# Expert weights in 16 KB runs, and expert outputs combined as gated float32r pairs

## The chip, the cores and the metric

The kernel runs on one core of a Trainium2 chip. The metric is the device time of one execution in microseconds (us), as the median of three runs.

## The reference

256 tokens of 1024 channels, float32, go through two blocks of two layers each. The first block's layers have two attention branches and a feed-forward part; the second block's layers have a mixer (retention, differential attention, gated linear attention) and then a mixture of experts, which is where the change acts:

```python
N_EXPERTS = 32
TOP_K = 2
D_EXPERT = 512
...
    def expert_block(args):
        toks, gts, e = args
        xb = h_pad[toks]
        u = jax.nn.silu(xb @ w_gate[e]) * (xb @ w_up[e])
        return (u @ w_down[e]) * gts[:, None].astype(xb.dtype)
```

Each token goes to two of 32 experts. An expert has a gate and an up matrix of 1024 x 512 and a down matrix of 512 x 1024. Its output rows are multiplied by the tokens' gates and added up for each token.

## The kernel before

**Weights.** All weights come through eight slots of 16 KB per partition, 2 MB each. `add` lists the tiles in the order of use, `pump` issues their DMAs on SyncE's queue (SP) in that order as long as a slot is free, and `done(name)` gives a slot back when the last product of a tile stands on TensorE (PE). `reserve(n)` holds n slots back. An expert's gate, up and down matrix are one tile each: w_eg, w_eu and w_ed in the trace. The source of each is laid out by `kp` (L592), "(k p) n -> p k n": partition p gets rows p, 128 + p, 256 + p and so on. So a partition's 16 KB come as eight runs of 2 KB (gate, up) or four runs of 4 KB (down).

**Experts in pairs.** `second_moe` goes through 16 pairs of experts. Each expert has 64 places, so the places of a pair fill 128 partitions. The two experts of a pair run side by side in the two column halves of PE's array. In the loop over i, PE's work stands in this order: the gate products of pair i (`two("g", ...)`), `combine` of pair i-1, the up products, `place` for pair i+1, and the down products.

**place.** `hot(i)` makes a one-hot matrix of tokens and places, once times the norm's factor of each token (`on`) and once times the gates (`ohg`). `place` gathers the tokens: for each of eight chunks of 128 channels, and for two halves of the tokens, it loads a 128 x 128 block of x as the stationary matrix and moves `on` through it. Here x is read by `x_chunk(t, k)`, 128 channels that lie side by side. Then two transposes turn `ohg` into `oT`. Between the two halves of the gathers stand four transposes of `u_`, the hidden activations of pair i (`turn_u`, L1958).

**combine.** `evac_y` (L1815, L1816) copies the pair's two output banks to SBUF, one on ScalarE (ACT) and one on VectorE (DVE), and `combine` multiplies them by `oT` in float32, four products of 128 x 512, into four banks that hold the sum over all pairs. The last pair's outputs are multiplied by a gain first and added on top.

**Past the places.** Ahead of pair 8 (`PAST`), `past_places` runs a loop (L1841) over blocks of tokens that found no place; in it the experts' weights are fetched by tiles of its own, OV, whose gathers use `oh`. In the profiled execution layer 0's loop has no pass and layer 1's has one.

**How it appears in the trace.** A float32 product is two instructions on PE, each with a weight load of its own (PEld); a float32r product is one. Buffers of the same pool share names: `qwh` holds placed tokens, `qwl` the outputs on their way to the combination, `C` stands for constants (the identity, ones), `bank` for PSUM. `macc` holds sums of modulation columns, which `mod_tail` turns by products with one column of ones.

Of the kernel before, what the change touches and what calls it, by code (L numbers as in the profile page):

```python
# [67 lines left out]
def constants():  # L68
# [20 lines left out]
    for lv in range(7):  # L89
# [27 lines left out]
       ("kv_a_norm_g", 2), ("b_gate", 16), ("norm1_g_2", 8), ("norm2_g_2", 8), ("b_mod_2", 48),  # L117
# [17 lines left out]
def build(ctx, tc, I, out, cols, cols2, dbg=None):  # L135
# [16 lines left out]
    def warm(n):  # L152
        """keeps the tensor engine's clock up through a wait on other engines"""
        p = bank()
        for _ in range(n):
            mm(p[:, :128], ident, ident, True, True)
# [11 lines left out]
    # ---- slots of 16 KB per partition: weights in the order of use, and large work tiles  # L168
# [11 lines left out]
    def pump():  # L180
        while st["issued"] < len(stream) and st["live"] + max(st["work"], st["reserve"]) < NSLOT:
            name, src, k, n, split = stream[st["issued"]]
            t = big.tile([128, k, n], F, name="w_" + name, tag="slot", bufs=NSLOT)
            if split == "turns":
                # a pair's two tiles in parts, by turns
# [7 lines left out]
            else:  # L193
                # the very first in parts, so that its products start early
# [27 lines left out]
    # ---- weights as float32r pairs, a few parts ahead of their products  # L222
# [71 lines left out]
    def tok_part(name, kk, c0, c1, ah, al, k, outs, start, stop):  # L294
        """outs[t] += A[t-th 128 rows] @ W[kk, c0:c1]; A is held transposed (ah + al)."""
        wh, wl = gran(name, kk, c0)
        n = c1 - c0
        for t in range(2):
            mm3(outs[t], ah[:, k, t * 128:(t + 1) * 128], al[:, k, t * 128:(t + 1) * 128],
                wh[:, :n], wl[:, :n], start, stop)  # L300

    def chan_part(name, kk, c0, c1, bh, bl, k, banks, start, stop):
        """banks hold [128 channels, 2, 256 tokens]; one 128-wide chunk of W after another."""
# [9 lines left out]
    # ---- constants and small parameters  # L313
# [55 lines left out]

    def load_c():  # L370
        return load_col(I["c_2"])
# [17 lines left out]
    # ---- pieces  # L389
# [8 lines left out]
    def rstd(ss, n, late=False):  # L398
# [6 lines left out]
        # from the exponent's half, three steps of Newton  # L405
# [15 lines left out]
    def to_pair(hi, lo, src, scale=None):  # L421
        """src (PSUM or SBUF) times a column or constant, as a float32r pair."""
# [11 lines left out]
    def norm_steps(src, dg, n, hi, lo, A, B=None):  # L434
        """hi + lo [128, chunk, 256] = (rows of src, times diag) transposed, times A (plus B)."""
# [26 lines left out]
    def x_stats(steps=False):  # L462
        """1 / rms of x's rows, or the steps to it"""
# [19 lines left out]
    def x_hat(dst):  # L483
        """x normed without gain, as chunks"""
# [10 lines left out]

    def row_of(r):
        """[128, 2], token 128t + p at [p, t] -> the row of 256 on every partition."""
# [7 lines left out]
    def bcast_row(col):  # L505
        """[128, 8] with channel 128k + p at [p, k] -> the row of 1024 on every partition."""
# [12 lines left out]
    class Post:  # L519
        """x += rmsnorm(acc) * gain, one half of the columns after the other; acc[t][half] are banks."""  # L520
# [12 lines left out]
        def add(self, sq=None):  # L533
            """sq: acc still lacks this factor of each row."""
# [26 lines left out]
    def mod_tail(keep=0):  # L561
        while len(mod_late) > keep:
            l, s, acc = mod_late.pop(0)
            p = bank()
            for c in range(4):
# [25 lines left out]
    # ---- the order of the weights  # L591
# [55 lines left out]
    # ---- softmax attention, units of [128 queries, 2, 256 keys]  # L647
# [59 lines left out]
    def first_layer(l):  # L707
# [5 lines left out]
        # the norm's factor of each row is left out here and multiplied in after the products  # L713
# [17 lines left out]
        for i, a, b in IN_TILES:  # L731
# [3 lines left out]
            for k in range(8):  # L735
# [8 lines left out]
                if i == 0 and k == 3:  # L744
                    # the latents, transposed as pairs; their norms' factors come after their products
# [23 lines left out]
        # grouped attention: norms of q and k and their rotary, on 10 heads of 64  # L769
# [31 lines left out]
        # up projections of the latents  # L801
# [26 lines left out]
        free(1)  # CT  # L828
        # rotary parts of the latent heads: 8 of q, one of k
# [17 lines left out]
        # gates  # L847
# [36 lines left out]
        # grouped attention: pairs of heads (p, p + 4), keys block-diagonal over the two kv heads  # L884
# [94 lines left out]
        free(1)  # M1  # L979
        drain()  # L980
        # branches, channels on partitions
# [38 lines left out]
        free(1)  # MG  # L1020
# [5 lines left out]
        # feed forward, 512 hidden channels at a time; the norm's factor r of each row is left out of its  # L1026
        # input and multiplied in after it, as r * r
# [54 lines left out]
    # ---- second block  # L1082
# [6 lines left out]
    def load_second():  # L1089
        nc.sync.dma_start(router, kp(I["router_w_2"]))  # L1090
# [4 lines left out]
    # rotary tables of the positions  # L1095
# [7 lines left out]
    def tables():  # L1103
# [8 lines left out]
        # the routing's bias plus the half of sigmoid(z) = tanh(z / 2) / 2 + 1/2  # L1112
# [49 lines left out]
    def stream_second(l):  # L1162
# [7 lines left out]
        for i in range(NE // 2):  # L1170
            for nm, src, k, n in (("g", I["w_gate_2"], 8, 512), ("u", I["w_up_2"], 8, 512), ("d", I["w_down_2"], 4, 1024)):
                for e in (2 * i, 2 * i + 1):
                    add("e%s%d_%d" % (nm, l, e), kp(src[l, e]), k, n, "turns" if nm in TURNS and i == NE // 2 - 1 else None)

    def head_norm(src, g, e, gate, dest):
        """dest = rmsnorm over e of src [128, g, e] times gate, in three pieces."""
# [18 lines left out]
    def silu_gate(src, gain, dest):  # L1195
        """dest [128, 512] = silu(src) * gain, for a gain given as its half, in two pieces."""
# [8 lines left out]
    def second_mix(l):  # L1205
# [10 lines left out]
        # ---- gated linear attention: projections  # L1216
# [31 lines left out]
        # gains of the differential heads: on the turned dimensions in the rotary tables, on the others  # L1248
        # with the transposition
# [27 lines left out]
        # log decay per token and channel  # L1277
# [24 lines left out]
        # gates times gains, ahead of their use  # L1302
# [10 lines left out]
        def qk_evac(s):  # L1313
            """q or k of the differential heads, normed and turned."""
# [24 lines left out]
        # decays of the levels  # L1339
# [78 lines left out]
        # ---- gated linear attention: scores level by level  # L1418
# [56 lines left out]
        # retention beside it, its tiles where q and k of the differential heads were  # L1475
# [98 lines left out]
        free(1)  # HT  # L1574
        drain()
        # ---- output projection, a pair of chunks after another as they come
# [21 lines left out]
        free(2)  # c2, DA  # L1598
# [4 lines left out]
        dve.scalar_tensor_tensor(a2, ms(4), 1.0, V(l, "norm2_g_2"), op0=OP.add, op1=OP.mult)  # L1603
# [14 lines left out]
        free(2)  # MX, MT  # L1618
# [4 lines left out]
    def list_past(cnt, pl3, wg3, nblk_i, eid_i, ov):  # L1623
        # an expert's blocks: one for each CAP tokens begun past the first CAP, at most three
# [31 lines left out]
    def second_moe(l):  # L1656
# [5 lines left out]
        def turn(k0, on_act):  # L1662
            p = bank()
            for k in (k0, k0 + 1):
                for t in range(2):
                    o = (k - k0) * 256 + t * 128
                    pe.transpose(p[:, o:o + 128], x_chunk(t, k), ident)  # L1667
# [20 lines left out]
        def quarter(tag):  # L1688
            """2 KB; the buffers that hold parts of weights elsewhere"""
            return wk.tile([128, 512], F, name="q" + tag, tag=tag, bufs=NSPLIT)  # L1690
        # ---- routing
# [59 lines left out]
        # ---- places: how many earlier tokens chose the same expert  # L1751
# [14 lines left out]
        # ---- tokens past an expert's 64 places: blocks of 64, listed by expert  # L1766
# [3 lines left out]
        def hot(i):  # L1770
            """one-hot of the pair's 2 x 64 places, times the norm's factors and times the gates."""
# [9 lines left out]
            return on, og  # L1781

        def place(oh, og, between=None):
            """the placed tokens, normed, modulated and transposed; the gated places, transposed."""
            hg = []
            for k0 in (0, 4):
# [3 lines left out]
                for k in range(k0, k0 + 4):  # L1790
                    o = p[:, (k - k0) * 128:(k - k0 + 1) * 128]
                    for t in range(2):
                        mm(o, x_chunk(t, k), oh[:, t], t == 0, t == 1)
# [9 lines left out]
            for t in range(2):  # L1803
                pe.transpose(p[:, t * 128:(t + 1) * 128], og[:, t], ident)  # L1804
            oT = t2((128, 2, 128), name="oT")
            act.activation(oT, p[:, :256].rearrange("p (t q) -> p t q", t=2), AF.Copy)
            return hg, oT

        def evac_y(py, last=False):
            y = [quarter("wl"), quarter("wl")]  # L1810
            if last:
                for h in range(2):
                    dve.tensor_tensor(y[h], py[h], g2_[:, h * 512:(h + 1) * 512], op=OP.mult)
                return y
            act.activation(y[0], py[0], AF.Copy)  # L1815
            dve.tensor_copy(y[1], py[1])  # L1816
# [4 lines left out]
        def combine(i, oT, y):  # L1821
            """the sum over the experts stays in four banks; the last pair's comes on top of it"""
            if not acc:
                acc.extend([bank(), bank()] for _ in range(2))
            for h in range(2):
                sl = slice(h * 512, (h + 1) * 512)
                for t in range(2):
                    if i < NE // 2 - 1:
                        mm(acc[t][h], oT[:, t], y[h], i == 0)
                        continue  # L1830
                    c = bank()
                    mm(c, oT[:, t], y[h], True, True)
# [4 lines left out]
        def past_places():  # L1837
            """the blocks past the places, one expert at a time"""
            OV = [slot("OV", [128, 2, 2048]) for _ in range(2)]
            nblk = nc.values_load(nblk_i[0:1, 0:1], min_val=0, max_val=NBLK - 1)  # L1840
            with tc.For_i(0, nblk, 1) as iv:  # L1841
# [3 lines left out]
                # 64 places; even chunks of the width go through the array's left half, odd ones through the  # L1845
                # right, and the halves are added as they are transposed
# [191 lines left out]
```

## Time and profile before

| what | value |
|---|---|
| three runs, us | 2164.03, 2168.88, 2169.59 |
| median, us | 2168.88 |
| profiled execution, us (its span) | 2165.9 |
| PE busy | 2056.2 us, 95% |
| DVE, ACT, GpSimd busy | 46%, 35%, 11% |
| DMA | 620.85 MB, mean 287 GB/s |

The span is that of one execution taken with the profiler; no other time is given for that execution. The share of busy time is an average: the first block's layers are bound by PE alone, while in the expert stages (971 to 1449 us and 1646 to 2149 us of the span) DMA moves weights all the time too.

### The profile page before, as it was taken

Reading aid. Unit: us, or ns where it says so; the run is one execution under the profiler, and the core shown is the slowest. Engines: PE = TensorE matmul, PEld = TensorE weight load, DVE = VectorE, ACT = ScalarE, POOL = GpSimd, SP = SyncE. Lnnn points to the kernel's source line nnn. Section 1 sums busy time; section 2 is a strip of 40 time slices with the busy share of each in tenths; the row PEclk is TensorE's granted clock in tenths of the full one; section 3 lists DMA queues with packets and bytes.
Section 4 is the critical chain, followed back from the end, with each engine's and each line's share of the span. In section 5 each row is a group of like instructions: output and inputs, shape, how many; then the busy total and the mean of one; then the engine's idle time right before and its main releaser. Section 6 shows DMA issues by size and latency. Waiting matters only on the chain. (4 is left out here: it accounts for less than half of the span.)

```text
span 2165.9 us, 28855 instructions
## 1 busy us (share of the span) xinstructions
PE 2056.2 (95%) x11394; PEld 1365.7 (63%) x11394; DVE 993.0 (46%) x1867; ACT 766.4 (35%) x1595; POOL 249.0 (11%) x309
## 2 busy tenths in 40 slices
PE   8999999999999989999999599998999999779999
PEld 6888999788899877774444244436685444333443
DVE  5767878776788867762110011115775111101112
ACT  6555655665565555431111011105452111101110
POOL 1211000021100014420000000002521000000000
PEclk9999999999999999999999799999999999989999
DMA  6545877454568732479999999994457999989998
GB/s 226 210 156 196 308 283 279 173 194 148 202 221 319 271 135 78 146 282 350 393 395 394 351 395 392 393 392 166 156 195 278 391 395 395 392 307 395 395 391 328
DMA packets 269950, 620.85 MB, mean 287 GB/s; under 512 B 9691, under 2 KB 14709, under 8 KB 269557
## 3 DMA queue, kind: packets, MB, share of 16 engines
q1 hardware_dynamic: 268660, 614.78, 76.4%
q10 hardware_dynamic: 1152, 4.20, 0.5%
q8 instruction: 91, 1.49, 0.3%
q14 instruction: 47, 0.38, 0.0%
HBM read 617.91 MB, written 1.05 MB: 286 GB/s over the span
## 5 line engine op out<-in xcount | busy, mean ns | idle before, releaser
L150 PE MATMUL bank<-U,wh 128*128 128x256 f32 x1536 | 287.5, 289 | 0.5 <-DVE U L428 0.4
L150 PE MATMUL bank<-w_eg,qwh 128*64 128x512 f32 x1024 | 230.2, 596 | 29.8 <-DMA w_ed<-in_w_down 25.4
L150 PEld LDWEIGHTS bank<-U,wh 128*128 128x128 f32 x1536 | 239.9, 190 | 8.4 <-issue 5.3
L150 PE MATMUL bank<-w_ed,uT 128*64 128x512 f32 x1024 | 229.6, 598 | 2.4 <-DMA w_ed<-in_w_down 2.1
L150 PE MATMUL bank<-w_eu,qwh 128*64 128x512 f32 x1024 | 227.4, 595 | 0.0
L150 PE MATMUL bank<-U,wl 128*128 128x256 f32 x768 | 218.6, 285 | 4.8 <-DVE wl L269 4.8
L1799 ACT ACTIVATE qwh<-bank,modc,a 128x128 f32<-128x128 f32 x128 | 58.5, 457 | 384.7 <-PE bank L150 354.0
L150 PEld LDWEIGHTS bank<-w_eg,qwh 128*64 128x64 f32 x1024 | 74.3, 138 | 179.5 <-issue 170.5
L150 PEld LDWEIGHTS bank<-w_eu,qwh 128*64 128x64 f32 x1024 | 77.1, 137 | 145.1 <-issue 138.3
L150 PE MATMUL bank<-wh,H 128*128 128x512 f32 x512 | 163.9, 395 | 0.0
L150 PEld LDWEIGHTS bank<-w_ed,uT 128*64 128x64 f32 x1024 | 71.3, 137 | 137.2 <-issue 133.3
L150 PE MATMUL bank<-wh,HT 128*128 128x512 f32 (+1 forms) x448 | 155.7, 402 | 0.6 <-ACT wh L257 0.6
L150 PEld LDWEIGHTS bank<-U,wl 128*128 128x128 f32 x768 | 146.0, 190 | 6.2 <-DVE wl L269 6.0
L150 PEld LDWEIGHTS bank<-on,x 128*128 128x128 f32 x1024 | 120.7, 194 | 26.7 <-issue 24.3
L150 PE MATMUL bank<-on,x 128*128 128x128 f32 x1024 | 129.4, 280 | 2.1 <-ACT on L1779 2.1
L584 DVE SCALAR_TENSOR_TENSOR macc<-w_mod,cact,macc 128x512 f32<-128x512 f32 x168 | 127.0, 756 | 0.0
L1776 POOL TENSOR_TENSOR ohg<-oh,wgt 128x256 f32<-128x256 f32 x32 | 20.3, 634 | 893.0 <-DVE oh L1774 893.0
L150 PE MATMUL bank<-qwl,oT 128*128 128x512 f32 (+1 forms) x264 | 120.5, 605 | 0.7 <-ACT qwl L1902 0.7
L150 PEld LDWEIGHTS bank<-wh,H 128*128 128x128 f32 x512 | 96.5, 188 | 21.7
L1934 ACT ACTIVATE sg<-bank 128x512 f32<-128x512 f32 x32 | 19.1, 597 | 253.3 <-PE bank L150 253.3
L257 ACT ACTIVATE wh<-w_dn 128x512 fp32r<-128x512 f32 x128 | 80.8, 631 | 74.9 <-PE bank L150 71.6
L1797 DVE TENSOR_SCALAR qwh<-bank,a,modc 128x128 f32<-128x128 f32 x128 | 52.5, 410 | 118.6 <-ACT qwh L1799 118.6
(524 smaller groups left out, 3425.2 us busy)
## 6 DMA issues: line engine op xcount, KB each, us to landing
w_eg<-in_w_gate SPq DMA_DIRECT2D x60, 2048.0 KB
w_eu<-in_w_up SPq DMA_DIRECT2D x60, 2048.0 KB
w_ed<-in_w_down SPq DMA_DIRECT2D x60, 2048.0 KB
w_mod<-in_w_mod SPq DMA_DIRECT2D x24, 2048.0 KB
w_up<-in_w_ffn_up SPq DMA_DIRECT2D x16, 2048.0 KB
w_dn<-in_w_ffn_down SPq DMA_DIRECT2D x16, 2048.0 KB
w_gate<-in_w_in SPq DMA_DIRECT2D x8, 2048.0 KB
w_D<-in_w_in SPq DMA_DIRECT2D x6, 2048.0 KB
```

The source lines that it names most:

```text
L150: pe.matmul(o, a, b, start=start, stop=stop, skip_group_check=True)
L257: act.activation(hi[:, :n], src, AF.Copy)
L584: dve.scalar_tensor_tensor(acc, w[:, k], cact[:, k:k + 1], acc, op0=OP.mult, op1=OP.add)
L1776: pool.tensor_tensor(og, oh, wg3[:, :, A][:, :, :, None].to_broadcast([128, 2, 2, 64]), op=OP.mult)
L1797: dve.tensor_scalar(hg[k], o, a2[:, k:k + 1], b2[:, k:k + 1], op0=OP.mult, op1=OP.add)
L1799: act.activation(hg[k], o, AF.Identity, scale=a2[:, k:k + 1], bias=b2[:, k:k + 1])
L1934: act.activation(sg, pg, AF.Silu)
```

## The change

The weights of the experts, of the loop's tiles and of the router are laid out by `rows_of`, "(p k) n -> p k n": partition p gets rows 8p to 8p + 7 (or 4p to 4p + 3), one run of 16 KB. Only the last pair's down tiles keep `kp`. So chunk k now holds channels k, 8 + k, 16 + k and so on, and what meets these weights is read in that order: x by `x_run` with a step of eight elements, `u_` with a step of four, the modulation columns by eight products of 64 strided columns.

The gates leave the transposed matrix: `oT` is the plain one-hot matrix in float32r, which holds it exactly, and two products of one column bring the gates of the places to a column `gp`. The outputs times `gp` are kept as a pair of float32r tiles, high and low part, and `combine` makes eight float32r products in place of four float32 ones. The combination of the pair ahead of the loop is made before the loop.

```diff
+    def x_run(t, k):
+        return x[:, t, k::8]
...
+            if s in (6, 7, 8, 9):
+                h = slice((s % 2) * 64, (s % 2) * 64 + 64)
+                for k in range(8):
+                    mm(p[h, k:k + 1], acc[:, k::8], ones[:, 0:1], True, True)
+                j = s // 2
+                dve.tensor_tensor(modc[l][h, j * 8:j * 8 + 8], p[h, :8], moe_vec[h, l, j - 2], op=OP.add)
+                continue
...
+    def rows_of(ap):
+        return ap.rearrange("(p k) n -> p k n", p=128)
...
-        nc.sync.dma_start(router, kp(I["router_w_2"]))
+        nc.sync.dma_start(router, rows_of(I["router_w_2"]))
+        load_moe_vec()
...
-                    add("e%s%d_%d" % (nm, l, e), kp(src[l, e]), k, n, "turns" if nm in TURNS and i == NE // 2 - 1 else None)
+                    add("e%s%d_%d" % (nm, l, e), (kp if nm == "d" and i == NE // 2 - 1 else rows_of)(src[l, e]), k, n, "turns" if nm in TURNS and i == NE // 2 - 1 else None)
...
-                    pe.transpose(p[:, o:o + 128], x_chunk(t, k), ident)
+                    pe.transpose(p[:, o:o + 128], x_run(t, k), ident)
...
-                        mm(o, x_chunk(t, k), oh[:, t], t == 0, t == 1)
+                        mm(o, x_run(t, k), on[:, t], t == 0, t == 1)
...
-                pe.transpose(p[:, t * 128:(t + 1) * 128], og[:, t], ident)
-            oT = t2((128, 2, 128), name="oT")
+                pe.transpose(p[:, t * 128:(t + 1) * 128], oh[:, t], ident)
+            for t in range(2):
+                mm(p[:, 256:257], og[:, t], ones[:, 0:1], t == 0, t == 1)
+            oT, gp = t2((128, 2, 128), R, name="oT"), small(1)
...
-        def evac_y(py, last=False):
-            y = [quarter("wl"), quarter("wl")]
+        def evac_y(py, gp, last=False):
+            y = [(quarter("wl", R), quarter("wl", R)) for _ in range(2)]
+            for h in range(2):
+                if last:
+                    s = t2(name="yg")
+                    dve.scalar_tensor_tensor(s, py[h], gp, g2_[:, h * 512:(h + 1) * 512], op0=OP.mult, op1=OP.mult)
+                    to_pair(*y[h], s)
+                else:
+                    to_pair(*y[h], py[h], gp)
...
-                        mm(acc[t][h], oT[:, t], y[h], i == 0)
+                    mm(c, oT[:, t], y[h][0], i in (0, NE // 2 - 1))
+                    mm(c, oT[:, t], y[h][1], False)
...
             if i == PAST:
+                combine(*pend)
+                pend = None
                 past_places()
...
-                        pe.transpose(p[:, k * 128:(k + 1) * 128], u_[:, k * 128:(k + 1) * 128], ident)
+                        pe.transpose(p[:, k * 128:(k + 1) * 128], u_[:, k * 128:(k + 1) * 128] if last else u_[:, k::4], ident)
```

`to_pair` is an older helper, which the change now calls with the column `gp` as the scale:

```python
    def to_pair(hi, lo, src, scale=None):
        ...
            act.activation(hi, src, AF.Copy, scale=scale)
            dve.scalar_tensor_tensor(lo, src, scale, hi.bitcast(F), op0=OP.mult, op1=OP.subtract)
```

**Where the instructions stand.** On PE, between the up products of pair 1 and its down products in layer 0, this stood before (`w_eu`, `w_ed`: weights of an expert; `u_`: the hidden activations):

```order
L150 MATMUL bank<-w_eu_3_10243,qwh 64x512
L150 MATMUL bank<-on,x 128x128 x8
L1958 MATMUL bank<-C,u__10458 128x128 x4
L150 MATMUL bank<-on,x 128x128 x8
L1804 MATMUL bank<-C,ohg 128x128 x2
L150 MATMUL bank<-w_ed_2_10327,uT 64x512
```

At the same place stands now:

```order
L150 MATMUL bank<-w_eu_3_10284,qwh 64x512
L150 MATMUL bank<-on,x 128x128 x8
L1989 MATMUL bank<-C,u__10511 128x128 x4
L150 MATMUL bank<-on,x 128x128 x8
L1828 MATMUL bank<-C,oh 128x128 x2
L150 MATMUL bank<-C,ohg 128x1 x2
L150 MATMUL bank<-w_ed_2_10368,uT 64x512
```

The gathers and the transposes keep their number and their place (that they read with a step doesn't show in these rows); two products of one column are added, and the two transposes take the plain one-hot matrix.

On PE at the entry of the loop in layer 0, between the last down products of pair 7 and the loop's body, this stood before:

```order
L150 MATMUL bank<-w_ed_15_11071,uT 64x512
L1840 TENSOR_LOAD nblk_i
L1841 COMPARE_AND_BRANCH
L1841 UNCONDITIONAL_BRANCH x2
L2034 BRANCH_PREFETCH_HINT
L150 MATMUL bank<-oh,x 128x64 x16
```

At the same place stands now:

```order
L150 MATMUL bank<-w_ed_15_11184,uT 64x512
L150 MATMUL bank<-qwl,oT 128x512 x8
L1869 TENSOR_LOAD nblk_i
L1870 COMPARE_AND_BRANCH
L1870 UNCONDITIONAL_BRANCH x2
L2065 BRANCH_PREFETCH_HINT
L150 MATMUL bank<-oh,x 128x64 x16
```

The combination of pair 7, eight products now, moved from behind pair 8's gate products to the place ahead of the loop.

## Rows read from the trace of the kernel before

**Rows 1.** The page: the span, and busy time of PE by its share.

```profile
span 2165.9 us, 28855 instructions
...
PE 2056.2 (95%) x11394; PEld 1365.7 (63%) x11394; DVE 993.0 (46%) x1867; ACT 766.4 (35%) x1595; POOL 249.0 (11%) x309
```

**Rows 2.** Layer 0's expert stage by windows: busy us (instructions), clock, DMA share, GB/s.

```profile
971.00:1204.00 233.00, 231.49 (x1146) 101.79 (x1144) 39.19 (x100) 35.70 (x77) 5.02 (x8) 1.00 1.00 377
1204.00:1229.50 25.50, 0.06 (x4) 0.02 (x2) 0.78 (x2) 0.00 (x0) 0.00 (x0) 0.60 0.90 343
1229.50:1449.00 219.50, 219.50 (x1056) 92.94 (x1058) 28.52 (x60) 29.10 (x64) 9.41 (x11) 0.99 1.03 389
```

**Rows 3.** PE's waits in layer 0's expert stage: us, times, longest.

```profile
PE bank L150 <- DMA w_ed<-in_w_down: 27.5, 2, 25.4
PE bank L150 <- DMA w_eg<-in_w_gate: 1.5, 1, 1.5
```

**Rows 4.** PE's waits in layer 1's expert stage.

```profile
PE bank L150 <- DMA OV<-in_w_gate: 21.5, 1, 21.5
PE bank L150 <- DMA w_eg<-in_w_gate: 2.4, 2, 1.6
```

**Rows 5.** PE's timeline over one pair, layer 0: start, us, instructions.

```profile
1020.45 7.09 PE L150 MATMUL bank<-w_ed,uT 128*64 128x512 f32 x32
1027.37 7.04 PE L150 MATMUL bank<-w_eg,qwh 128*64 128x512 f32 x32
1034.34 3.70 PE L150 MATMUL bank<-qwl,oT 128*128 128x512 f32 x8
1037.97 7.09 PE L150 MATMUL bank<-w_eu,qwh 128*64 128x512 f32 x32
1044.98 2.05 PE L150 MATMUL bank<-on,x 128*128 128x128 f32 x16
1046.87 0.60 PE L1958 MATMUL bank<-C,u__10581 128*128 128x128 f32 x4
...
1049.10 0.38 PE L1804 MATMUL bank<-C,ohg 128*128 128x128 f32 x2
1049.41 1.08 PE L150 MATMUL bank<-w_ed,uT 128*64 128x512 f32 x4
```

**Rows 6.** Windows with DMA of 2 KB rows, 4 KB rows, and long rows.

```profile
1045.00:1050.00 5.00, 5.00 (x44) 4.55 (x44) 1.72 (x4) 1.86 (x4) 0.00 (x0) 1.00 1.04 387
1060.00:1065.00 5.00, 5.00 (x20) 1.73 (x17) 0.00 (x0) 0.89 (x2) 0.00 (x0) 1.00 1.02 408
794.20:796.40 2.20, 0.00 (x0) 0.00 (x0) 2.20 (x4) 1.74 (x5) 0.00 (x0) 0.88 1.01 420
```

**Rows 7.** DMA queues from 794.2 to 796.4: packets, MB, share.

```profile
q10 hardware_dynamic: 86, 0.75, 80.4%
```

**Rows 8.** SP's timeline around the loop of layer 0.

```profile
1204.20 8.39 SPq L196 DMA_DIRECT2D w_ed<-in_w_down  x2
1229.30 1.00 SPq L196 DMA_DIRECT2D w_eg<-in_w_gate  x2
```

**Rows 9.** PE's timeline of float32r products of 512 columns.

```profile
940.69 0.63 PE L150 MATMUL bank<-wh,MT 128*128 128x512 f32 x2
941.16 0.40 PE L150 MATMUL bank<-wl,MT 128*128 128x512 f32 x1
```

**Rows 10.** PE's groups by form: one-column products.

```profile
L150 PE MATMUL bank<-C,macc 128*128 128x1 f32 x192 | 22.6, 240 | 0.0
```

**Rows 11.** DVE's timeline after pair 1's down products.

```profile
1027.61 0.69 DVE L1816 COPY qwl<-bank 128x512 f32<-128x512 f32 x1 [5.43 <-PE bank L150]
```

**Rows 12.** Three lines of DVE reductions: ns, and elements read.

```profile
L1740 DVE TENSOR_REDUCE sm<-mx x2: 185/186/188, 964.2 to 1638.5; 128x8 f32<-128x32 f32 x2
...
L1643 DVE TENSOR_REDUCE sm<-ow x2: 420/420/421, 976.7 to 1652.6; 128x8 f32<-128x256 f32 x2
...
L1729 DVE TENSOR_REDUCE sm<-tb x2: 261/264/267, 963.2 to 1637.4; 128x8 f32<-128x64 f32 x2
```

More of the change, by code (lines that the diff above doesn't have):

```diff
@@ L116 @@
 VEC = [("pre_mix_g", 8), ("post_mix_g", 8), ("pre_ffn_g", 8), ("post_ffn_g", 8), ("q_a_norm_g", 3),
-       ("kv_a_norm_g", 2), ("b_gate", 16), ("norm1_g_2", 8), ("norm2_g_2", 8), ("b_mod_2", 48),
+       ("kv_a_norm_g", 2), ("b_gate", 16), ("norm1_g_2", 8), ("b_mod_2", 48),
        ("diff_q_g_2", 1), ("diff_k_g_2", 1)]
@@ L368, in put_col, with load_moe_vec @@
         return col
+    moe_vec = cst.tile([128, DEPTH, 3, 8], F, name="moe_vec")
+    def load_moe_vec():
+        for l in range(DEPTH):
+            nc.sync.dma_start(moe_vec[:, l, 0], I["norm2_g_2"][l].rearrange("(p k) -> p k", p=128))
+            for i in range(2):
+                nc.sync.dma_start(moe_vec[:, l, 1 + i], I["b_mod_2"][l, (3 + i) * D:(4 + i) * D].rearrange("(p k) -> p k", p=128))
     def load_c():
@@ L1602, in second_mix @@
         ra = t2((128, 8, NE), name="ra")
-        dve.scalar_tensor_tensor(a2, ms(4), 1.0, V(l, "norm2_g_2"), op0=OP.add, op1=OP.mult)
+        dve.scalar_tensor_tensor(a2, ms(4), 1.0, moe_vec[:, l, 0], op0=OP.add, op1=OP.mult)
         pool.tensor_tensor(ra, router, a2[:, :, None].to_broadcast([128, 8, NE]), op=OP.mult)
@@ L1686, in second_moe, with quarter @@
         turn(6, True)
-        def quarter(tag):
-            return wk.tile([128, 512], F, name="q" + tag, tag=tag, bufs=NSPLIT)
+        def quarter(tag, dt=F):
+            return wk.tile([128, 512], dt, name="q" + tag, tag=tag, bufs=NSPLIT)
         p = bank()
@@ L1780, in hot, with place @@
             dve.tensor_scalar(on[:, 1], oh[:, 1], rx[:, 1:2], None, op0=OP.mult)
-            return on, og
-        def place(oh, og, between=None):
+            return on, oh, og
+        def place(on, oh, og, between=None):
             hg = []
@@ L1803, in place @@
             for t in range(2):
-                pe.transpose(p[:, t * 128:(t + 1) * 128], og[:, t], ident)
-            oT = t2((128, 2, 128), name="oT")
+                pe.transpose(p[:, t * 128:(t + 1) * 128], oh[:, t], ident)
+            for t in range(2):
+                mm(p[:, 256:257], og[:, t], ones[:, 0:1], t == 0, t == 1)
+            oT, gp = t2((128, 2, 128), R, name="oT"), small(1)
             act.activation(oT, p[:, :256].rearrange("p (t q) -> p t q", t=2), AF.Copy)
-            return hg, oT
-        def evac_y(py, last=False):
-            y = [quarter("wl"), quarter("wl")]
[L1811 to L1816, printed above, removed]
+            dve.tensor_copy(gp, p[:, 256:257])
+            return hg, (oT, gp)
+        def evac_y(py, gp, last=False):
[7 more added lines that the diff above has]
+                    to_pair(*y[h], py[h], gp)
             return y
@@ L1827, in combine @@
                 for t in range(2):
+                    c = acc[t][h] if i < NE // 2 - 1 else bank()
+                    mm(c, oT[:, t], y[h][0], i in (0, NE // 2 - 1))
+                    mm(c, oT[:, t], y[h][1], False)
                     if i < NE // 2 - 1:
-                        mm(acc[t][h], oT[:, t], y[h], i == 0)
                         continue
-                    c = bank()
-                    mm(c, oT[:, t], y[h], True, True)
                     dve.tensor_tensor(x[:, t, sl], x[:, t, sl], c, op=OP.add)
@@ L1857, in past_places @@
                     for t in range(2):
-                        mm(p[:, k * 64:(k + 1) * 64], x_chunk(t, k), oh[:, t], t == 0, t == 1)
+                        mm(p[:, k * 64:(k + 1) * 64], x_run(t, k), oh[:, t], t == 0, t == 1)
                 for k in range(8):
@@ L1874, in half @@
                     cnt_[0] += 1
-                    w = src[l, bass.ds(e, 1)].rearrange("o (k p) n -> p (o k) n", p=128)
+                    w = src[l, bass.ds(e, 1)].rearrange("o (p k) n -> p (o k) n", p=128)
                     nc.sync.dma_start(b, w[:, j * k:(j + 1) * k, :])
@@ L1890, in past_places @@
                     for k in range(4):
-                        mm(p[:, j * 256 + k * 64:j * 256 + k * 64 + 64], a[:, k * 128:(k + 1) * 128], two_i, True, True)
+                        mm(p[:, j * 256 + k * 64:j * 256 + k * 64 + 64], a[:, k::4], two_i, True, True)
                 sg, uT = t2((128, 256), name="sg"), t2((128, 4, 64), name="uT")
@@ L1974, in second_moe @@
                 reserve(4)
-            pend = (i, oT, evac_y(py, last))
+            pend = (i, oT[0], evac_y(py, oT[1], last))
             h2, oT = nxt
```

## The prediction

> **What bounds the kernel now.** I read the page first. TensorE (PE) works through 2056.2 of 2165.9 us [rows 1], so the time is PE's work plus what PE waits for, and the change can act in no other way. Then the busy time of the expert stages [rows 2]. In layer 0 PE is busy for 231.49 of 233 us up to the end of pair 7, idle for 25.5 us, and busy without a gap for 219.5 us, while the DMA engines move 377 and 389 GB/s at a share of 1.0 or more wherever PE works. So both run flat out, and DMA is slightly behind: what it lacks is paid at one place. The list of PE's waits shows where: 25.4 us for w_ed and 2.1 + 1.5 us of small waits in layer 0 [rows 3]; 21.5 us for the loop's own tile OV and 2.4 us for w_eg in layer 1 [rows 4].
>
> The timeline of one pair without a wait [rows 5] gives its parts. From one w_ed to the next are 28.96 us: down 6.92, gate 6.97, combine 3.63, up 7.01, place 4.43. In the place sixteen gather instructions take 1.89 us, 0.112 to 0.118 us each. DMA needs longer. The stretch that moves 2 KB rows (gate, up) runs at 387 GB/s, the one with 4 KB rows (down) at 408 [rows 6], so the pair's tiles take 8.39 MB / 387 + 4.19 MB / 408 = 31.96 us. That is 3.0 us a pair behind PE, 24 us in eight pairs, which is the 25.4 us at the loop's entry: SP issues two w_ed tiles at 1204.20, as pair 7 frees their slots, and its next DMA not before 1229.30, when all that was issued has landed [rows 8]. At 390 GB/s these 25 us hold 4.7 tiles, the two new ones and 2.7 of lag.
>
> **The change part by part.**
>
> *Combine.* Eight float32 instructions take 3.63 us. float32r instructions of the same width follow each other every 0.235 us (two in 0.47) [rows 9]: eight take 1.88. Saved: 1.75 us a pair, 28.0 a layer.
>
> *Gate column.* Two products of one column, four instructions, join each place. The kernel has such instructions on macc: 22.6 us / 192 = 0.118 us [rows 10]. So +0.47 a pair, +7.5 a layer.
>
> *Evacuation.* Two passes become four (ACT with a scale, then a subtraction on DVE, for each half). A copy of this size takes DVE 0.69 us and starts at 1027.61 [rows 11]; combine reads the tiles at 1034.34 [rows 5]. So 1.3 to 1.5 us more are hidden behind the next gate phase, with about 5 us to spare; without that cover they would cost 1.5 us a pair. Only the last pair has none: there one multiplication is followed by a copy and a subtraction, about +1.3 us a layer, +2.6 in all. The combine of pair 7 now stands ahead of the loop, where PE waits for DMA: it costs nothing there.
>
> *Runs of 16 KB.* From rows of 2 KB and 4 KB: 16 engines at 387 and 408 GB/s spend 84.7 ns on a 2 KB packet and 160.6 ns on a 4 KB one, that is 75.9 ns per 2 KB and 8.8 ns for the packet. A 16 KB run then takes 616 ns, 425 GB/s, and a pair 29.6 us, if the last step is as straight as the first. The third stretch bears it out as far as it goes: four fifths of its DMA time are 86 packets that hold 0.75 MB, 8.7 KB each, and it moves 420 GB/s [rows 6, 7]. The bounds are 394 GB/s (no gain) and 425. By the Trainium skill ("DMA: Bandwidth & Descriptors", Why small descriptors are slow) a packet carries about three cycles beside one for each 32 bytes; that alone would give 4% for 2 KB and 2% for 4 KB, a pair of some 30.9 us, less than the rows here give.
>
> *The price: strided reads.* PE now loads x with a step of eight elements, 32 bytes, in all 512 gather instructions of a layer (32 a place, 16 places) and in 16 transposes of the turn, and u_ with a step of 16 bytes in 60 transposes. That is 588 loads of 128 columns a layer, 36 a pair. The gathers go at the pace of their loads, since each moves 128 columns and loads 128. No strided read by PE is in this trace. Bounds: nothing, if PE's load port doesn't mind; and the price that a strided read has on another engine. DVE reduces 32 contiguous elements in 186 ns and 256 in 420 [rows 12], 1.045 ns an element, so 219 ns for 64. The reduction at L1729 reads 64 with a step of 16 bytes: 264 ns. So 0.70 ns more for each, 1.74 ns in all. At 1.74 ns a load of 128 columns takes 0.223 us and not 0.112: excess 0.111 us. I take that, since it is the only row with such a step, and the same memory is read; the step of 32 bytes has no row. The lower figure if DVE's surplus alone is added is 128 x 0.70 = 0.089.
>
> The Trainium skill speaks against the change here: "SBUF — State Buffer", Specifications, says that SBUF has lines of 16 bytes and wants at least two hits on a line for full bandwidth, for whichever engine reads, and "Advanced Engine Details and Errata", Memory Cachelines, says the same. A step of 16 or 32 bytes hits each line once, so by that rule the load pays, as DVE's row does; the page gives no price. By the rule the sum is the one below, without it that of the first rival.
>
> *Small.* In the loop of layer 1 the strided gathers lie behind the wait for OV; gs_ and us_ (16 instructions) add 1.8 us. The eight sets of modulation columns that are interleaved take eight products of 64 strided columns each instead of four of 128: 64 instructions more at 0.112, +7.1 us, in a stage where PE waits for little. Router and moe_vec loads are a few KB, ahead of their use by hundreds of us: nothing.
>
> *Sum.* PE per layer: -28.0 + 7.5 + 588 x 0.111 = +44.8. A pair becomes 28.96 - 1.75 + 0.47 + 36 x 0.111 = 31.7 us, above DMA's 29.6: PE is then the bound, DMA no longer lags, and at the loop only the two tiles issued at pair 7's end are still to come, 2 x 2.097 MB / 425 = 9.9 us. So layer 0 gets back 25.4 - 10 + 3.6 = 19.0, layer 1 21.5 - 10 + 2.4 = 13.9. Total: 2 x 44.8 + 7.1 + 1.8 + 2.6 - 32.9 = +68 us. The profiled execution's span is 2165.9, the median of the runs 2168.9; 3 us are within their spread, so I add the sum to the median: **2237 us**. Its own range: excess 0.089 takes off 28 (2209), waits that shrink by half as much add 16 (2254).
>
> **The rivals.**
>
> *Strided loads are free.* The pair is then 27.7 us on PE, under DMA's 29.6, so DMA stays the bound but lags 1.9 a pair instead of 3.0. PE: 2 x (-20.5) = -41. Waits: 1.08 x 8 = 8.6 less at each loop and 6.0 of small ones: -23.2. With +2.6: -62, **2107 us** (2095 to 2125). For it: the load is an engine's own path, and no row shows it slowed. Against it: DVE's row. It decides by the excess of a load: 1256 such loads in all times the excess equals the other terms at 0.057 us, half of what I take; below that the kernel is faster.
>
> *Half the excess.* About 0.05 to 0.06 us a load: pair 29.7, waits as in the forecast, sum -10 to +10: about **2168**.
>
> *Runs of 16 KB move no faster and loads are free.* Then DMA binds throughout as before: PE's saving of 1.3 us a pair only lengthens its waits, sum about 0 in both layers, **2168**. Against it: 387, 408 and 420 GB/s rise with the run.
>
> **How the numbers follow.** Forecast 0.58, free loads 0.27, half 0.09, no gain in DMA 0.06. A measurement here can tell about 0.3% (6.5 us) from no change. Slower: 0.58 and a third of the half case, 0.61; faster: 0.27 and a third, 0.30; same: the rest, 0.09. The range goes from 2100 to 2254, as cases of both signs hold it; the forecast's own is 2209 to 2254.
>
> **What would show it.** Gathers from `x` 0.22 us apart and a place near 8.9 us if the loads pay, 0.112 and 4.9 if not. Combine: eight instructions in 1.9 us. Windows within the expert stage above 415 GB/s if PE keeps DMA busy; in the forecast DMA's share falls below 1 between pairs. PE's idle time at the loop near 10 us in both layers. Wrong would make me: gathers that keep their pace; idle time at the loop that stays above 20; or a combine that now waits for its pairs (an idle stretch ahead of `qwl,oT`).

## The result and the profile after

The changed kernel takes 2235.91 us (median of four runs, 2234.65 to 2239.45) against 2166.45 us of before, measured beside it: a ratio of 1.0333, 95% interval 1.0320 to 1.0345. The forecast was 2237 us. The profiled execution's span is 2233.8 us, 67.9 more than before.

One pair on PE in layer 0, which answers to [rows 5] (start, length, instructions):

```profile
1034.10 2.13 PE L150 MATMUL bank<-qwl,oT 128*128 128x512 f32 x8
1036.15 7.09 PE L150 MATMUL bank<-w_eu,qwh 128*64 128x512 f32 x32
1043.17 4.10 PE L150 MATMUL bank<-on,x 128*128 128x128 f32 x16
1047.11 0.64 PE L1989 MATMUL bank<-C,u__10511 128*128 128x128 f32 x4
1047.59 3.98 PE L150 MATMUL bank<-on,x 128*128 128x128 f32 x16
1051.41 0.38 PE L1828 MATMUL bank<-C,oh 128*128 128x128 f32 x2
1051.62 0.50 PE L150 MATMUL bank<-C,ohg 128*128 128x1 f32 x4
1052.06 7.09 PE L150 MATMUL bank<-w_ed,uT 128*64 128x512 f32 x32
...
1068.00 7.09 PE L150 MATMUL bank<-w_eu,qwh 128*64 128x512 f32 x32
```

The lengths that count are from the start of a group to the start of the next. Combine takes 2.05 us, not 3.63. Sixteen gathers take 3.94 and 3.82 us, 0.24 us each, not 1.89. The gate column takes 0.44, and the two transposes of the one-hot matrix ahead of it 0.21 where those of the gated one took 0.31. The four transposes of `u_`, which now read with a step of 16 bytes, take 0.48, and took 0.44. From one pair to the next pass 31.85 us (1036.15 to 1068.00), not 28.96. The DMA side, in a stretch of ten microseconds in which it has enough to do, and in the stage (windows as in [rows 2], and the queues of the stretch as in [rows 7]):

```profile
1100.00:1110.00 10.00, 10.00 (x45) 5.19 (x44) 0.69 (x1) 0.00 (x0) 0.00 (x0) 1.00 1.00 426
```

```profile
q1 hardware_dynamic: 291, 4.24, 99.4%
```

```profile
995.30:1250.10 254.80, 254.80 (x1178) 136.47 (x1177) 45.56 (x115) 40.82 (x84) 5.17 (x8) 1.00 0.91 379
1250.10:1254.60 4.50, 2.52 (x10) 1.39 (x8) 2.67 (x4) 0.75 (x2) 0.61 (x1) 1.00 0.28 58
1254.60:1490.00 235.40, 235.37 (x1080) 123.31 (x1082) 33.55 (x72) 34.54 (x71) 8.87 (x10) 1.00 0.96 395
```

The runs of 16 KB arrive at 426 GB/s, but over the two halves of the stage DMA's share is now 0.91 and 0.96, since PE is the slower of the two, and PE is busy throughout. At the loop PE is idle for 1.7 us where it was idle for 25.4, and that is not for a DMA; first PE's timeline up to pair 8's gate products of layer 0, then the longest entry in the list of PE's waits there:

```profile
1250.21 0.50 PE L150 MATMUL bank<-qwl,oT 128*128 128x512 f32 x1
1251.00 1.90 PE L150 MATMUL bank<-qwl,oT 128*128 128x512 f32 x7 [0.28 <-DVE qwl L437]
1254.63 7.09 PE L150 MATMUL bank<-w_eg,qwh 128*64 128x512 f32 x32 [1.73 <-DVE on L1804]
```

```profile
PE bank L150 <- DVE on L1804: 1.7, 1, 1.7
```

### The profile page after: what moved, and what is told of

Same layout as the page of the kernel before. It is cut to its first block, busy times and chain, and to the rows that moved or that the text cites. A ratio compares the mean times of both kernels' runs of the same rounds, so it can differ in the third digit from the quotient of the medians.

```text
span 2233.8 us, 29304 instructions
## 1 busy us (share of the span) xinstructions
PE 2172.2 (97%) x11586; PEld 1533.6 (69%) x11586; DVE 1022.3 (46%) x1933; ACT 792.8 (35%) x1629; POOL 249.0 (11%) x309
## 5 line engine op out<-in xcount | busy, mean ns | idle before, releaser
L150 PEld LDWEIGHTS bank<-on,x 128*128 128x128 f32 x1024 | 250.1, 336 | 26.5 <-issue 24.3
L150 PE MATMUL bank<-on,x 128*128 128x128 f32 x1024 | 258.3, 407 | 2.0 <-ACT on L1803 2.0
L150 PE MATMUL bank<-w_eg,qwh 128*64 128x512 f32 x1024 | 225.4, 592 | 2.1 <-DVE on L1804 1.7
L150 PEld LDWEIGHTS bank<-w_eu,qwh 128*64 128x64 f32 x1024 | 70.9, 137 | 139.5 <-issue 138.5
L1800 POOL TENSOR_TENSOR ohg<-oh,wgt 128x256 f32<-128x256 f32 x32 | 20.9, 653 | 938.9 <-DVE oh L1798 938.9
L437 DVE SCALAR_TENSOR_TENSOR qwl<-bank,sm,qwl 128x512 fp32r<-128x512 f32 x60 | 45.0, 751 | 171.8 <-ACT qwl L436 167.9
L257 ACT ACTIVATE wh<-w_up 128x512 fp32r<-128x512 f32 x128 | 80.3, 631 | 77.5 <-PE bank L150 71.8
```

The source lines that it names most:

```text
L150: pe.matmul(o, a, b, start=start, stop=stop, skip_group_check=True)
L257: act.activation(hi[:, :n], src, AF.Copy)
L437: dve.scalar_tensor_tensor(lo, src, scale, hi.bitcast(F), op0=OP.mult, op1=OP.subtract)
L1800: pool.tensor_tensor(og, oh, wg3[:, :, A][:, :, :, None].to_broadcast([128, 2, 2, 64]), op=OP.mult)
```

## The experiments

Two theories stood against each other after this profile. One: a load of the stationary matrix pays for its step in SBUF. The other: the gathers are slowed by something that came with the change, such as the longer runs that DMA writes beside them. `u_`, with a step of 16 bytes at nearly the old pace, left open from which step on a load pays. Of the longer edits only the lines that matter are shown; `...` stands where lines are left out.

**A ladder of steps.** In the kernel before, the gathers of later pairs read x with other steps.

```diff
-                        mm(o, x_chunk(t, k), oh[:, t], t == 0, t == 1)
+                        c = k * 128 * (step <= 1)
+                        mm(o, x_all[:, c:c + 127 * step + 1:step], oh[:, t], t == 0, t == 1)
...
+STEPS = (1, 1, 1, 2, 2, 3, 3, 4, 4, 4, 6, 6, 8, 8, 16, 16)
```

> The kernel before, with the gathers of pairs 3 to 15 reading x with a step of 2, 3, 4, 6, 8 or 16 elements instead of side by side (other channels are gathered, the number and form of the instructions stay). Theory (a strided load pays by the lines of SBUF it touches, and 16 bytes is the border that is still nearly free, as the u_ transposes of the changed kernel suggest, 4 in 0.48 us): gathers 0.11 to 0.12 us apart for steps 1, 2, 3 and 4, and 0.24 us for 6, 8 and 16. Rival 1 (each access to a new 16-byte line pays, as the forecast had it): step 4 already at 0.22 to 0.25 us. Rival 2 (it isn't the step, but the longer runs that DMA writes meanwhile): 0.112 us for all steps.

Sixteen gathers on PE's timeline, for steps of 1, 2, 3, 4, 6, 8 and 16 elements in this order:

```profile
1017.63 2.05 PE L150 MATMUL bank<-on,x 128*128 128x128 f32 x16
...
1046.59 2.15 PE L150 MATMUL bank<-on,x 128*128 128x128 f32 x16
...
1104.89 3.04 PE L150 MATMUL bank<-on,x 128*128 128x128 f32 x16
...
1166.77 4.00 PE L150 MATMUL bank<-on,x 128*128 128x128 f32 x16
...
1283.29 3.83 PE L150 MATMUL bank<-on,x 128*128 128x128 f32 x16
...
1348.35 4.07 PE L150 MATMUL bank<-on,x 128*128 128x128 f32 x16
...
1414.33 3.75 PE L150 MATMUL bank<-on,x 128*128 128x128 f32 x16
```

2.05, 2.15, 3.04, 4.00, 3.83, 4.07, 3.75 us: the price follows the number of 16-byte stretches that a load touches. Step 2 touches one for every two elements and costs 5%; step 3 touches three for four elements; from step 4 on it is one for each element, and a longer step costs no more. So rival 1 holds and my theory falls: 16 bytes already pay in full. Rival 2 falls too, since here DMA writes runs of 2 and 4 KB as before. Its time, 2195.79 us, mixes the steps and says little.

**8 KB runs, step of 16 bytes.** The changed kernel with gate and up rows in two halves.

```diff
+        return ap.rearrange("(h p k) n -> p h k n", h=2, p=128)
...
-        return x[:, t, k::8]
+        h, k = divmod(k, 4)
+        return x[:, t, h * 512 + k:(h + 1) * 512:4]
```

> The changed kernel with gate and up weights in two runs of 8 KB per partition instead of one of 16 KB, so that x is read with a step of 4 elements (16 bytes) instead of 8; the modulation columns take four products of 128 columns with step 4. The result is the reference's. Theory (a step of 16 bytes costs PE's load next to nothing, 32 bytes twice the time): the pair takes PE 27.9 us; DMA at about 420 GB/s for 8 KB runs needs 29.8 us a pair and binds, the wait at the loop comes back to about 16 us (layer 0), and the time is near 2107 us, 0.973 of before. Rival (16 bytes cost as 32 do): gathers 0.24 us apart, pair 31.9, time near 2230 us, 1.03.

2211.59 us, 1.0209 (1.0194 to 1.0224; here and below the time over that of the kernel before, with its 95% interval). The rival holds, and the gathers are as slow as with 32 bytes:

```profile
1064.01 4.00 PE L150 MATMUL bank<-on,x 128*128 128x128 f32 x16
1067.85 0.63 PE L1998 MATMUL bank<-C,u__10614 128*128 128x128 f32 x4
1068.32 3.88 PE L150 MATMUL bank<-on,x 128*128 128x128 f32 x16
```

Between them stand the four transposes with the same step in 0.47 us. So `u_` had misled me: a transposition's load with a step of 16 bytes keeps its pace, a float32 product's doesn't. The time is still 24 us under the changed kernel's: a pair takes 31.63 us and not 31.85, 7 us in 32 pairs, and the router's products of layer 0 start 9 us earlier; the rest wasn't followed.

**x side by side again.** The changed kernel with other channels in the gathers.

```diff
-        return x[:, t, k::8]
+        return x[:, t, k * 128:(k + 1) * 128]
```

> The changed kernel with x read side by side again in gathers, turn and loop (other channels than the weights want); 16 KB runs, u_ with step 4, modulation columns and combination as changed. Theory (the step of 32 bytes is what costs): gathers 0.112 us apart, pair 27.8 us on PE, DMA at 427 GB/s needs 29.5 and binds, wait at the loop about 14 us, time near 2116 us, 0.977 of before. Rival (the gathers are slowed by what DMA writes beside them, or the combination costs): gathers 0.24 apart, time stays near 2236 us.

2121.00 us, 0.9790 (0.9773 to 0.9807), 5 us from the forecast, with waits of 11.3 us at layer 0's loop and 15.7 at layer 1's. The routing goes by other numbers here, so the loop's one pass fell in layer 0. Sixteen gathers on PE, and a window of the expert stage:

```profile
1057.46 2.05 PE L150 MATMUL bank<-on,x 128*128 128x128 f32 x16
```

```profile
1080.00:1120.00 40.00, 40.00 (x224) 20.06 (x222) 6.91 (x16) 7.44 (x16) 0.65 (x1) 1.00 1.01 427
```

With the same runs beside them, at 427 GB/s, the gathers are fast again: the step alone makes them slow.

**Runs of 16 KB alone.** The kernel before with `rows_of` for the experts (and, by a second edit of the same kind, for the loop's tiles).

```diff
-                    add("e%s%d_%d" % (nm, l, e), kp(src[l, e]), k, n, "turns" if nm in TURNS and i == NE // 2 - 1 else None)
+                    add("e%s%d_%d" % (nm, l, e), (kp if nm == "d" and i == NE // 2 - 1 else rows_of)(src[l, e]), k, n, "turns" if nm in TURNS and i == NE // 2 - 1 else None)
...
```

> The kernel before with the expert weights in 16 KB runs and nothing else (x, u_ and the rest read side by side, so channels and weights don't match). Theory (the runs are worth 394 to 427 GB/s, and that is the gain the change gives away again): the pair stays 28.96 us on PE, DMA needs 29.5, the wait at the loop falls from 25.4 to about 6 us, the small waits go, time near 2123 us, 0.98 of before. Rival (the runs bring nothing by themselves, the waits went because PE got slower): waits at the loop above 20 us, time within 0.3% of before.

2107.14 us, 0.9731 (0.9713 to 0.9749). The wait at each loop is 10.0 and 10.3 us (6 expected) and the small waits are gone. This time is too good by a pass: with the other numbers no token stood past the places, so neither loop ran. In the kernel before the loop's pass makes the stretch from pair 7's to pair 8's up products 76.5 us long in layer 1 and 56.4 in layer 0; with those 20 us the time would be near 2127, by my estimate. The next two kernels have no such doubt.

**8 KB runs, and x copied in order once a layer.** GpSimd copies x into four tiles in the chunks' order beside the routing, and VectorE's last step over a set of modulation columns writes them in order. The float32r outputs move to other buffers to make room.

```diff
+                pool.tensor_copy(xp[t][h], x[:, t, h * 512:(h + 1) * 512].rearrange("p (q k) -> p k q", k=4))
...
-                        mm(o, x_run(t, k), on[:, t], t == 0, t == 1)
+                        mm(o, xp[t][k // 4][:, k % 4], on[:, t], t == 0, t == 1)
```

> The changed kernel with 8 KB runs for gate and up, but no strided load on TensorE except in the turn and u_: GpSimd copies x once a layer into four tiles in the order of the chunks (beside the routing), the gathers load those side by side, and VectorE's last step over a set of modulation columns writes them in the new order. The result is the reference's. Theory (the strided loads are the whole price of the change, the runs its gain): gathers 0.112 to 0.118 us apart, pair 27.9 us on PE, DMA 29.8 us a pair binds, wait at the loop about 17 us, small waits gone; time near 2113 us, 0.976 of before. Rival (copy, reordering and the new tiles' waits cost as much as they save): time above 2150 us, with idle time ahead of the first gathers.

2115.42 us, 0.9765 (0.9748 to 0.9783). In the windows DMA is back at a share of 1.01, with 8 KB and 16 KB runs mixed, and PE's waits at the loops are DMA's again:

```profile
1040.00:1080.00 40.00, 40.00 (x224) 20.08 (x222) 6.63 (x15) 7.40 (x16) 0.65 (x1) 1.00 1.01 423
```

```profile
PE bank L150 <- DMA w_ed<-in_w_down: 16.9, 1, 16.9
PE bank L150 <- DMA OV<-in_w_gate: 15.2, 1, 15.2
```

So with 8 KB runs, and without strided loads for the gathers and the modulation columns, the change is 51 us faster than before; as it was made, it is 69 slower.

**Step of two.** Gate and up in four runs of 4 KB; h=4 in the layout.

```diff
-        return x[:, t, k::8]
+        h, k = divmod(k, 2)
+        return x[:, t, h * 256 + k:(h + 1) * 256:2]
...
+        return ap.rearrange("(h p k) n -> p h k n", h=4, p=128)
```

> The changed kernel with gate and up weights in four runs of 4 KB per partition, so that x and the modulation columns are read with a step of two elements (8 bytes); down stays at 16 KB and u_ at a step of four. The result is the reference's. Theory (a load pays for each 16-byte line that it touches beyond the first 64 lines, so two elements a line are nearly free): gathers 0.12 to 0.125 us apart, pair 28.2 us on PE, DMA 30.4 us a pair binds, wait at the loop about 19 us; time near 2125 us, 0.981. Rival (any step in the gathers makes them slow): gathers above 0.2 us, pair near 31, time near 2200 us.

2122.62 us, 0.9803 (0.9787 to 0.9820). Sixteen gathers take 1.99 us from start to start (1043.16 to 1045.15), a pair 28.0, and PE waits 20.5 us at layer 0's loop:

```profile
1043.16 2.15 PE L150 MATMUL bank<-on,x 128*128 128x128 f32 x16
```

Two elements for each 16 bytes are as good as free, without a copy.

**The changed kernel without the pairs.** The combination alone is put back; that of pair 7 keeps its place ahead of the loop.

```diff
...
-                    mm(c, oT[:, t], y[h][0], i in (0, NE // 2 - 1))
-                    mm(c, oT[:, t], y[h][1], False)
+                    mm(c, oT[:, t], y[h], i in (0, NE // 2 - 1))
...
```

> The changed kernel with the combination as before (float32, gated places transposed, no gate column), layouts and steps as changed. The result is the reference's. Theory (the changed kernel is bound by PE in the expert stages, so PE's saving in the combination counts in full there): the pair takes 31.85 + 1.58 - 0.44 = 33.0 us, time near 2270 us, 1.048 of before. Rival (the combination's part is hidden or spent on the longer evacuation): time within 0.3% of the changed kernel's 2236 us.

2267.6 us, 1.0474 (1.0453 to 1.0496): 32 us above the changed kernel; the pair takes 33.05 us (1032.62 to 1065.67) and not 31.85. In 32 pairs that would be 38 us, so under a PE bound most of the saving counts; where the rest stays wasn't tried.

**The pairs alone.** The kernel before with the new combination, and layouts and reads as they were; as an edit of the changed kernel:

```diff
-        return x[:, t, k::8]
+        return x[:, t, k * 128:(k + 1) * 128]
...
-        return ap.rearrange("(p k) n -> p k n", p=128)
+        return kp(ap)
```

> The kernel before with the combination as changed (float32r pairs, one-hot matrix, gate column, combination ahead of the loop) and all layouts and reads as before. The result is the reference's. Theory (before, DMA runs flat out in both halves of the expert stage, so what PE saves becomes waiting): the pair takes PE 27.8 us, DMA still 32.0, the wait at the loop grows from 25 to about 33 us and waits for weights appear after it; time 2160 to 2167 us, within 0.3% of before. Rival (PE's saving counts): 36 us less, near 2130 us, 0.983.

2168.93 us, 1.0013 (1.0003 to 1.0023). PE needs 1.2 us a pair less, and it comes back as waiting: in layer 0 the first pairs pass in 27.72 us (28.96 before), the next in 29.0, and the two ahead of the loop in 31.9 (up products start at 1124.59, 1156.48 and 1188.42). That is the pace that the prediction worked out for DMA, 31.96 us a pair. Of the whole run's waits for weights the list shows:

```profile
PE bank L150 <- DMA OV<-in_w_gate: 19.7, 1, 19.7
PE bank L150 <- DMA w_eg<-in_w_gate: 12.9, 11, 1.5
PE bank L150 <- DMA w_eu<-in_w_up: 8.0, 12, 0.7
```

23 small waits for gate and up weights, 20.9 us together, stand where there were 1.5 and 2.4 us for gate weights [rows 3, 4]. The list holds only a part of what is given back; the starts of the pairs show it whole. The wait at layer 0's loop did not grow as I expected (23.0 us of idle time behind the combination); the lack showed pair by pair instead.

**The copies on ScalarE.**

```diff
-                pool.tensor_copy(xp[t][h], x[:, t, h * 512:(h + 1) * 512].rearrange("p (q k) -> p k q", k=4))
+                act.activation(xp[t][h], x[:, t, h * 512:(h + 1) * 512].rearrange("p (q k) -> p k q", k=4), AF.Copy)
```

> The kernel with 8 KB runs and a copy of x in the order of the chunks, with the four copies on ScalarE behind its tanh in the routing instead of on GpSimd, where they took 4.27 us and held up VectorE's routing steps. The result is the reference's. Theory (PE's start on the first pair frees the slots, so a start 3 us earlier a layer counts in full): first gate products about 16.5 us behind the router's products instead of 19.5, time near 2109 us. Rival (DMA binds up to the loop, so an earlier start only lengthens the wait there): time within 0.2% of 2115 us, wait at the loop 20 us instead of 16.9.

2109.95 us, 0.9742 (0.9728 to 0.9756), the fastest kernel here that keeps the reference's arithmetic. It gained 5.5 us on the copies on GpSimd, although the first gate products came 18.4 us behind the router's, where they had been 19.5 and I had expected 16.5. Two starts that are 1.1 us earlier account for 2 of the 5.5 us; the rest is open, and small beside the spread (2108.05 to 2112.88 us here, 2112.06 to 2117.74 there).

**The same, with the old combination.** The edit is that of the kernel without the pairs, with its evacuation (`...` as above):

```diff
...
-                    to_pair(*y[h], py[h], gp)
...
+            act.activation(y[0], py[0], AF.Copy)
+            dve.tensor_copy(y[1], py[1])
```

> The same kernel as the other with copies on ScalarE, but with the combination as before the change (float32, gated places, no gate column). The result is the reference's. Theory (with DMA at 29.8 us a pair the pair's 29.0 us on PE leave DMA the bound up to the loop, and behind it, where tiles lie ahead, PE binds, so the pairs are worth 1.13 us x 8 there a layer): wait at the loop 6 to 9 us shorter, time about 15 us above the other, near 2124 us. Rival 1 (DMA binds behind the loop too): the same time within 0.2%. Rival 2 (PE binds everywhere): 33 us above.

2126.11 us, 0.9816 (0.9802 to 0.9830): 16.2 us above the other, as the theory had it. The wait at layer 0's loop is 8.5 us where the other's is 17.9, and at layer 1's 5.0 where the other's is 15.3: up to the loop what PE saves is waited away. Behind each loop the pairs make the other 9 us faster: there it counts.

**Modulation columns in order.** The changed kernel with VectorE writing these sets in order, so that PE loads 64 columns side by side.

```diff
-                    mm(p[h, k:k + 1], acc[:, k::8], ones[:, 0:1], True, True)
+                    mm(p[h, k:k + 1], acc[:, k * 64:(k + 1) * 64], ones[:, 0:1], True, True)
...
```

> The changed kernel with the eight interleaved sets of modulation columns put in order by VectorE's last step over them, so that PE loads 64 columns side by side instead of with a step of eight. The result is the reference's. Theory (these strided loads cost 1.1 us a set in the first layers): the 16 instructions of a set take about 1.1 us instead of 2.08, time near 2228 us. Rival (what the first layers lose lies elsewhere, in VectorE's or ScalarE's order or in the clock): time within 0.2% of 2236 us.

2224.18 us, 1.0275 (1.0260 to 1.0289), 11.7 below the changed kernel. The group of these 128 instructions on PE, in the changed kernel and then here:

```profile
L150 PE MATMUL bank<-C,macc 128*64 128x1 f32 x128 | 16.6, 259 | 0.0
```

```profile
L150 PE MATMUL bank<-C,macc 128*64 128x1 f32 x128 | 8.7, 198 | 0.0
```

A load of 64 columns pays for its step too; 8 of the 11.7 us are seen in these rows.

## Why the prediction held

The time came out 1 us from the forecast, and that is luck: errors of some 20 us on either side cancelled. The waits gave back 18 us more than I reckoned; the pairs, the loop and the first layers cost as much more.

- **Strided loads: right, and undersized.** The forecast took 0.223 us a load from VectorE's reduction; PE takes 0.24. 32 gathers a pair cost 4.08 us more, not 3.55. The kernels that read x side by side show that this is what turns faster into slower. The Trainium skill's rule ("SBUF — State Buffer", Specifications: lines of 16 bytes, two hits wanted on each) agrees with the ladder: two hits cost 5% at step 2, one hit doubles the time.
- **Transposes: wrong.** I charged 0.44 us a pair for those of u_ and 0.04 were paid. Those of the turn, charged 1.8 us a layer, follow each other every 0.11 to 0.12 us in the changed kernel too, with a step of 32 bytes.
- **Combine and gate column: right.** -1.58 for -1.75, and +0.44 for +0.47. With the transposes of the one-hot matrix (-0.10) the sum of a pair is +2.89, where I had +2.72.
- **Evacuation: right.** Within the pairs nothing waits for it; only at the loop and behind the last pair the combination waits, for 0.3 and 0.8 us in layer 0 (1.3 reckoned behind the last pair).
- **Runs of 16 KB: right.** 426 GB/s where a straight line through two rows gave 425.
- **The wait at the loop: the step that failed.** "At the loop only the two tiles issued at pair 7's end are still to come", 10 us in each layer. It is 1.7 us in layer 0, none of it for DMA, and in layer 1 no wait for OV is left. I had read SP's row at 1204.20 [rows 8] as the issue that pair 7's end sets free. It was late. Pair 7's up products, which set these slots free, had ended at 1192.5; SP was still in the row before, which ended at 1204.08:

```profile
1191.66 12.42 SPq L196 DMA_DIRECT2D w_eu<-in_w_up  x2
```

  In the changed kernel SP issues the same tiles as pair 7's up products end, 16 us before the down products do, and nothing in between:

```profile
1225.27 0.81 SPq L196 DMA_DIRECT2D w_eu<-in_w_up  x2
1234.35 0.80 SPq L196 DMA_DIRECT2D w_ed<-in_w_down  x2
1253.23 0.81 SPq L196 DMA_DIRECT2D w_eg<-in_w_gate  x2
```

  Two issues take 0.8 us here and took 8.39 and 12.42 before, while two tiles at 390 GB/s take 10.8: SP went at DMA's pace, and a row's start told of DMA's lag and not of a slot. So the layers got back 27.3 and 23.9 us and not 19.0 and 13.9. A wait also cost clock, which I had left out: while TensorE stood idle in layer 0's wait, its granted clock fell to a mean of 0.60 [rows 2], mostly the lower of its two levels (1.2 of 2.4 GHz), and the gate products behind it took 8.71 us, where they take 7.09 now.

```profile
1229.48 8.71 PE L150 MATMUL bank<-w_eg,qwh 128*64 128x512 f32 x32 [25.44 <-DMA w_ed<-in_w_down]
```

- **Loop's gathers: wrong, small.** With the wait for OV gone, nothing hides them: 32 took 3.95 us before and take 7.88. The products on gs_ and us_ take 1.9 us more, as reckoned (1.8).
- **First layers: undersized.** I had +7.1 for the modulation columns. The rows show +9.1, the kernel with them in order is 11.7 us faster.

Pairs 32 x 2.89 = 92.5, waits -51.2, columns +9.1, loop +5.8 make 56 of the 67.9 us. By the starts of the same products the expert stages grew by 41 us and not by the 47 of this sum: the lost clock behind the waits is a part of the difference. So more than the other 12 lies outside them, for the most part ahead of layer 0's: its router's products start 18.5 us later, where the columns' rows explain 9. The kernel without the pairs and the one with x side by side have the same columns, and there they start 12.8 and 12.9 us later. What the profiled execution has beyond that may be the clock, whose mean between its two levels (1.2 and 2.4 GHz) was lower on the way; here the changed kernel (0.92), then the one before (0.96):

```profile
700.00:825.00 125.00, 116.88 (x685) 104.21 (x684) 84.87 (x167) 67.24 (x127) 5.00 (x11) 0.92 0.58 208
```

```profile
690.00:808.00 118.00, 109.88 (x673) 98.49 (x672) 86.54 (x171) 68.08 (x128) 4.37 (x11) 0.96 0.63 229
```

Besides, the turn's transposes now wait 3.8 us for x in the two layers, of which every chunk needs both halves. How the remainder is divided wasn't tried.

## What to carry to other kernels

A layout that makes DMA's runs longer moves the interleaving to whoever reads the data next; price that read before the transfer, and if it is a stationary load in float32, keep at least two neighbours for each 16 bytes or copy the data in order once on an engine that has time. What a faster stage is worth depends on who binds it at that moment: the same float32r pairs were worth nothing, 16 and 32 us, under a DMA bound, a bound on DMA up to the loop only, and a bound on PE. Here a DMA's issue row that lasted 8 to 13 us, where 0.8 is enough, showed that DMA was behind, and its start said nothing of when the slot came free.

## What the runs showed of the hardware

- A float32 load of 128 stationary columns follows the last in 0.112 to 0.118 us at step 1 and in about 0.24 us from step 4 on, that is 1.9 ns for each 16-byte stretch that it touches; steps of 6, 8 and 16 cost no more than 4 (3.75 to 4.07 us for sixteen).
- The load of a transposition with a step of 16 or 32 bytes keeps a pace of 0.11 to 0.12 us. Why it is spared wasn't tried.
- DMA's rate rose with the run at every length that was tried: 387 GB/s at 2 KB, 408 at 4 KB, 423 with 8 and 16 KB mixed, 426 at 16 KB.
